# The convolution stage of a two-layer decoder trunk: gating, pivot and mean in PSUM, the first norm among the first products, warm-up products, 26 in place of 18 taps on TensorE

## The chip, the core and the metric

The kernel runs on one core of a Trainium2 chip. The metric is device time in microseconds (us) of one execution. TensorE (PE) multiplies, PEld is its weight load, VectorE (DVE), ScalarE (ACT) and GpSimd (POOL) do the elementwise work, SyncE (SP) issues most DMAs. [...]

## What is computed

A trunk of two layers on 512 tokens of 1024 channels, in float32. Only the first part of layer 0 is touched, the Conformer convolution module behind an RMS norm:

```python
def conformer_conv(h, w_pw1, b_pw1, w_dw, b_dw, ln_g, ln_b, w_pw2, b_pw2):
    u = h @ w_pw1 + b_pw1                     # h = rms_norm(x): 1024 -> 2048
    a, gate = jnp.split(u, 2, axis=-1)
    u = a * jax.nn.sigmoid(gate)
    u = lax.conv_general_dilated(u, w_dw[:, None, :], ..., padding=((30, 0),),
                                 feature_group_count=D_MODEL) + b_dw   # depthwise, causal, 31 taps
    u = jax.nn.silu(layer_norm(u, ln_g, ln_b))
    return u @ w_pw2 + b_pw2                  # added to x
```

Behind it come memory cross-attention, a SwiGLU FFN, and the second layer (differential attention, memory attention, FFN, final norm). Keys and values of the 256 memory tokens do not depend on the convolution, and the kernel computes those of both layers inside the convolution stage.

## The kernel before

Channels lie on the 128 partitions in eight blocks (`KT = 8`), the 512 tokens along the free axis. Each float32 product is three TensorE products: every operand is split into a rounded part (a cast on ACT) and a remainder (a subtraction, `lo`, on DVE or POOL), and `mm3` issues high by high, high by low, low by high (512 columns each). `weights` (L208) loads 128 columns of a matrix, 512 KB, through SP and splits it: cast `wh` at L213 on ACT, remainder `wl` at L215 on the engine given as `lo`.

The order of instructions on each engine is made when the program is built: a scheduler simulates the engines and takes the first ready instruction in program order. `tc.issue_after(x)` keeps the instructions of its block behind `x` on x's engine. At run time each engine works through its own list strictly in order, and semaphores hold an instruction until its inputs are there.

The convolution stage, in `conformer`:

- **Head.** Eight blocks `xT[t]` are loaded, scaled by the norm's gain and split (`Norm.take`: `xg`, cast on ACT L226, remainder on DVE L227). `gated(0)` makes the gate product `pg` of block 0 (8 input blocks, 24 products), squares `x` (ACT L309, sum on DVE L310), sums over channels on TensorE (`sums`, L117 to `ps_st`), then makes the other product `pa`. `spread` forms 1/rms: `rsqrt` takes a POOL power (L269) and one Newton step of three DVE operations (L275 to L277), four transposes (L121) broadcast it, and ACT copies it to `R`. All gating waits for `R`.
- **Gating** of block j (L368 to L371): DVE multiplies `pg` by `R` into `tg`; ACT takes the sigmoid `sg`; DVE multiplies `pa` by `R` into `u[j]` in SBUF (L370) and then forms `(u + bias) * sg` in place (L371), with two SBUF inputs.
- **Convolution** of block j, `conv(j)`: DVE adds tap after tap into a PSUM bank `ps_conv` (L405, one SBUF and one PSUM input); taps 1 to 6 (`POOL_TAPS`) go by ACT (L387) and POOL (L388) into `g`; for blocks 6 and 7 the taps listed in `PE_TAPS` go by TensorE, each tap as a diagonal matrix built on ACT (L398, two operations) and three products. L407 adds `ps_conv` and `g` into `u[j]`.
- **Layer norm.** `pivm` (all 1/1024) times `u[j]` on TensorE gives the mean of blocks 0 to 3 in `pm[0]` (called `ps_piv` in the trace). ACT copies twice that to SBUF as `piv`; `deviations` subtracts it (L414, blocks 0 to 5 on POOL, 6 and 7 on DVE), squares on ACT and adds into `ss` (L420). At the end `mq` (L447) is the mean of what is left, in SBUF; `ss` is corrected (L449), summed on TensorE, `rsqrt` with three Newton steps runs on DVE (L271 to L277), transposes to `ps_bc` broadcast it; `mq` is subtracted from every block (L458: blocks 0 to 2 POOL, 3 to 7 DVE), then L463 scales, ACT takes silu and L220/L221 split for the second pointwise product `ps_out`.
- **Fill.** `memory_kv` is a generator of 32 steps (`ps_mk`, `ps_mv` products); `FILL[j]` steps are taken after block j, and what is left comes after the last mean product `centre`. Its weights use POOL for `wl`.

PSUM has eight banks in this stage: ring 0 to 3 for the pointwise and memory products, 4 and 5 for `ps_conv`, 6 for `piv`, 7 for `st`.

## Time and profile before

| what | us |
|---|---|
| median of 3 runs (lowest to highest) | 1526.03 (1525.06 to 1527.97) |
| the profiled execution's own time | 1527.41 |
| its span, first to last instruction | 1525.6 |
| mean granted TensorE clock | 0.99 of full speed |
| start of the uninterrupted `ps_out` products, which end the stage | 241.84 |

The span is 1.8 us under the profiled execution's own time, and that execution is 1.4 us above the median. Times in the rows are microseconds from the first instruction unless marked ns. Busy matmuls overlap in the records, so the pace of TensorE is read from the chain of waits (a stretch divided by its count), not from the mean of one. [...]

### The profile page before, as it was taken

The numbers are of one execution on the slowest core, as the hardware profiler recorded it, in microseconds if no ns is written. First come the engines' busy times: TensorE is split into PE (matmuls) and PEld (weight loads), VectorE is DVE, ScalarE is ACT, GpSimd is POOL, SyncE is SP. The second block draws the span as 40 slices with busy tenths as digits, with TensorE's granted clock in tenths as the row PEclk, the third lists the DMA queues.
The fourth block names the chain that finished last, engine by engine and source line by source line (L and its number), as shares of the span: only waits on it lengthen the run. The fifth ranks groups of instructions, "written<-read, shape, count | busy, mean of one in ns | idle before, by whom it ended". The sixth has DMA issues, their size and how long they took to land.

```text
span 1525.6 us, 18451 instructions
## 1 busy us (share of the span) xinstructions
PE 1480.9 (97%) x7204; PEld 1213.1 (80%) x7204; DVE 905.2 (59%) x1369; ACT 607.5 (40%) x990; POOL 385.6 (25%) x218
## 2 busy tenths in 40 slices
PE   6999879999999999999999999999999999999998
PEld 4888758887888888888887878788878888888886
DVE  5999986555664345425569888765564533543444
ACT  6655746354343122222334555453443232222222
POOL 5999784310221022012000000011002201210212
PEclk9999999999999999999999999999999999999999
DMA  7454225211433332332323111232124223232321
GB/s 216 125 146 131 93 97 152 69 56 49 121 97 97 88 102 87 98 96 87 93 86 95 56 56 56 86 88 77 56 83 125 89 92 97 87 106 84 97 96 56
DMA packets 231815, 143.59 MB, mean 94 GB/s; under 512 B 5552, under 2 KB 217648, under 8 KB 231728
## 3 DMA queue, kind: packets, MB, share of 16 engines
q1 hardware_dynamic: 230432, 141.58, 31.3%
q8 instruction: 56, 0.92, 0.2%
q10 hardware_dynamic: 1296, 0.84, 0.2%
q14 instruction: 31, 0.25, 0.1%
HBM read 138.20 MB, written 4.19 MB: 93 GB/s over the span
## 4 chain that ended last, share of the span: by engine, by line
PE 88%; DVE 8%; issue 1%; ACT 1%; DMA 1%; POOL 0%; POOLq 0%; DVEq 0%; SPq 0%; ACTq 0%
PE ps_gu L117 32%; PE ps_out L117 9%; PE ps_down L117 8%; PE ps_fin L117 8%; PE ps_lin L117 5%; PE ps_pw L117 3%; PE ps_v L117 3%; PE ps_q L117 3%; PE ps_k L117 2%; PE ps_mv L117 2%; PE ps_mk L117 2%; DVE ps_conv L405 2%; PE ps_s L117 2%; PE ps_mo L117 2%; PE ps_ms L117 1%
## 5 line engine op out<-in xcount | busy, mean ns | idle before, releaser
L213 ACT CAST wh<-st 128x1024 fp32r<-128x1024 f32 (+1 forms) x254 | 263.4, 1041 | 598.3 <-issue 187.2
L117 PE MATMUL ps_gu<-xg,wh 128*128 128x512 f32 x1408 | 438.9, 392 | 0.0
L215 POOL TENSOR_TENSOR wl<-st,wh 128x1024 fp32r<-128x1024 f32 x100 | 258.4, 2590 | 670.5 <-ACT wh L213 637.2
L117 PEld LDWEIGHTS ps_gu<-xg,wh 128*128 128x128 f32 x1408 | 264.3, 188 | 63.0
L117 PE MATMUL ps_gu<-xg,wl 128*128 128x512 f32 x704 | 278.4, 395 | 0.0
L215 DVE TENSOR_TENSOR wl<-st,wh 128x1024 fp32r<-128x1024 f32 (+1 forms) x154 | 186.5, 1214 | 84.1 <-ACT wh L213 81.9
L117 PEld LDWEIGHTS ps_gu<-xg,wl 128*128 128x128 f32 x704 | 132.2, 188 | 28.5
L405 DVE SCALAR_TENSOR_TENSOR ps_conv<-u,wcol,ps_conv 128x499 f32<-128x499 f32 (+21 forms) x176 | 120.1, 730 | 5.3 <-PE ps_conv L117 2.0
L584 DVE TENSOR_TENSOR tu<-ps_gu,R 128x512 f32<-128x512 f32 x44 | 30.4, 691 | 140.0 <-PE ps_gu L117 139.9
L117 PE MATMUL ps_fin<-wh,a 128*128 128x512 f32 (+1 forms) x364 | 111.0, 386 | 0.0
L117 PE MATMUL ps_down<-a,wh 128*128 128x512 f32 x352 | 109.5, 394 | 0.0
L117 PE MATMUL ps_pw<-xg,wh 128*128 128x512 f32 x256 | 84.1, 407 | 12.0 <-ACT wh L213 8.9
L221 DVE TENSOR_TENSOR a<-ta,a 128x512 fp32r<-128x512 f32 x44 | 73.7, 1676 | 22.2 <-ACT a L220 22.2
L117 PE MATMUL ps_lin<-xg,wh 128*128 128x512 f32 x256 | 81.5, 395 | 0.0
L117 PE MATMUL ps_out<-mo,wh 128*128 128x512 f32 x256 | 80.6, 396 | 0.9 <-ACT wh L213 0.9
L117 PEld LDWEIGHTS ps_fin<-wh,a 128*128 128x128 f32 x364 | 67.7, 188 | 15.3
L117 PEld LDWEIGHTS ps_down<-a,wh 128*128 128x128 f32 x352 | 66.0, 188 | 15.2
L582 DVE TENSOR_TENSOR tg<-ps_gu,R 128x512 f32<-128x512 f32 x44 | 30.4, 691 | 76.1 <-PE ps_gu L117 70.2
L117 PE MATMUL ps_fin<-wl,a 128*128 128x512 f32 (+1 forms) x182 | 70.4, 387 | 0.0
L117 PE MATMUL ps_down<-a,wl 128*128 128x512 f32 x176 | 68.8, 394 | 0.0
L117 PEld LDWEIGHTS ps_pw<-xg,wh 128*128 128x128 f32 x256 | 49.0, 195 | 24.7 <-ACT wh L213 8.9
L117 PEld LDWEIGHTS ps_out<-mo,wh 128*128 128x128 f32 x256 | 47.3, 188 | 13.6 <-ACT wh L213 3.4
(256 smaller groups left out, 2517.6 us busy)
## 6 DMA issues: line engine op xcount, KB each, us to landing
st<-in_ffn_w_up_dram SPq DMA_DIRECT2D x44, 512.0 KB, 3.8
st<-in_ffn_w_gate_dram SPq DMA_DIRECT2D x44, 512.0 KB, 3.8
st<-in_ffn_w_down_dram SPq DMA_DIRECT2D x38, 512.0 KB, 3.8
st<-in_conv_w_pw_dram SPq DMA_DIRECT2D x24, 512.0 KB, 4.6
st<-in_mem_w_k_dram SPq DMA_DIRECT2D x16, 512.0 KB, 4.1
st<-in_mem_w_v_dram SPq DMA_DIRECT2D x16, 512.0 KB, 3.7
st<-in_mem_w_q_dram SPq DMA_DIRECT2D x16, 512.0 KB, 4.0
st<-in_mem_w_o_dram SPq DMA_DIRECT2D x16, 512.0 KB, 4.0
```

Source lines behind the costliest of these rows:

```text
L117: ins = nc.tensor.matmul(*args, **kw)
L213: A.copy(wh, st)
L215: (lo or V).tensor_tensor(wl, st, f(wh), op=ALU.subtract)
L221: (lo or V).tensor_tensor(l, src, f(h), op=ALU.subtract)
L405: V.scalar_tensor_tensor(acc[:, s:], u[j][:, :S - s], wt(s), acc[:, s:], op0=ALU.mult, op1=ALU.add)
L582: V.tensor_tensor(tg, pg, n.R, op=ALU.mult)
L584: V.tensor_tensor(tu, pu, n.R, op=ALU.mult)
```

## The change

Six edits, all in the convolution stage.

1. The second half of the gating stays in PSUM: `pa` is multiplied by `R` in place and L371's counterpart has one PSUM and one SBUF input.
2. `pm[0]` gets a bank of its own (ring 6, 7 for `piv`; `st` moves to bank 5, shared with `ps_conv`) and is no longer copied; all eight deviations are DVE operations that read it from PSUM, with the factor -2 in the instruction.
3. The mean is kept in PSUM: ACT copies `pm[1]` to `mq`, DVE puts the difference into `pm[0]`, and all eight final subtractions are DVE operations that read it there.
4. The first norm: the products of blocks 0 and 1 come before both gatings; `sums` comes after `pg` and six of eight input blocks of `pa`, `spread` after three more of block 1; its `rsqrt` runs on DVE with three Newton steps; the two weight remainders of block 0 go to DVE.
5. 48 products of 128 columns in bfloat16 on constants, into a PSUM bank that nothing reads, before the first products.
6. `PE_TAPS`: 10 taps in place of 6 for block 6, 16 in place of 12 for block 7. Taps 2, 4 and 6 of both blocks thereby leave ACT and POOL, tap 18 of block 6 and tap 30 of block 7 leave DVE.

```diff
--- before.py
+++ after.py
@@ -37,7 +37,8 @@
 FFN_GROUPS = [list(range(0, 8)), list(range(8, 16)), list(range(16, 22))]
 NEG = -1.0e30
 POOL_TAPS = [1, 2, 3, 4, 5, 6]
-PE_TAPS = {6: [0, 8, 10, 12, 14, 16], 7: [0, 8, 10, 12, 14, 16, 18, 20, 22, 24, 26, 28]}
+PE_TAPS = {6: [0, 2, 4, 6, 8, 10, 12, 14, 16, 18], 7: list(range(0, CW, 2))}
+WARM = 48
 FILL = [4, 5, 2, 2, 1, 2, 2, 6]
 getcontext().prec = 60
@@ -71,7 +72,7 @@
 MEMB = {"e": 4, "sq": 1, "mo": 16}
 FFN0B = {"tg": 3, "sg": 3, "tu": 4, "ta": 4, "sq": 2, "ctab": 2, "stab": "ctab", "lq": 2, "lpr": "lq", **TABLES}
 FFNB = {"tg": 3, "sg": 3, "tu": 4, "ta": 4, "sq": 2, "gf": 2, "xo": 8}
-CONV = {"mkf": 8, "piv": 2, "mq": "piv", "tg": 2, "sg": 2, "g": 2, "q": 2, "z": "tg", "s_": "sg", "dq": 2,
+CONV = {"mkf": 8, "mq": 1, "tg": 2, "sg": 2, "g": 2, "q": 2, "z": "tg", "s_": "sg", "dq": 2,
         "lss": 1, "msrc": 2, "mks": "msrc", "sq": "dq", "u": 8}
 SLOTS = {
     "c": CONV, "c2": CONV, "m0": {"mkf": 8, **MEMB}, "m1": {"fetch": 4, **MEMB}, "f0": FFN0B, "f1": FFNB,
@@ -87,7 +88,7 @@
 MEMP = {"lin": "01", "ms": "23", "out": "04152637", "": "4567"}
 FFNP = {"": "01234567"}
-CONVP = {"": "0123", "conv": "45", "piv": "6", "st": "7", "bc": "4", "out": "012356"}
+CONVP = {"": "0123", "conv": "45", "piv": "67", "st": "5", "bc": "4", "out": "012356"}
 BANKS = {
     "c": CONVP, "c2": CONVP,
     "m0": MEMP, "m1": MEMP, "f0": FFNP, "f1": FFNP,
@@ -320,12 +321,12 @@
             self.ps = bank("st", [P, NB, 2])
             return token_sums(self.ps, self.ss)
-        def spread(self):
+        def spread(self, eng=G):
             ps = self.ps
             v = small("nv", [P, NB])
             V.tensor_scalar(v, ps[:, :, 0], 1.0 / D, RMS_EPS, op0=ALU.mult, op1=ALU.add)
             self.r = tl("rs", [P, NB])
-            V.tensor_copy(self.r, rsqrt(v, NB))
+            V.tensor_copy(self.r, rsqrt(v, NB, eng))
             pb = bank("st")
             ins = broadcast_rows(self.r, pb)
             self.R = tl("R")
@@ -350,25 +351,50 @@
         for t in range(KT):
             nc.sync.dma_start(xT[t], xt[t * P:(t + 1) * P, :])
             if t == 0:
-                w0 = weights(conv_w_pw1[0][:, D:D + P], lo=G)
+                w0 = weights(conv_w_pw1[0][:, D:D + P])
             n0.take(t, xT[t])
+        warm = bank("piv")
+        for _ in range(WARM):
+            T.matmul(warm[:, :P], identb, mask, start=True, stop=True)
         def gated(j):
             pg, pa = bank("pw1"), bank("pw1")
-            linear(conv_w_pw1[0], KT + j, n0.xs, pg, lo=G, w=w0 if j == 0 else None)
+            W, lo = conv_w_pw1[0], V if j == 0 else G
+            wg = w0 if j == 0 else weights(W[:, (KT + j) * P:(KT + j + 1) * P], lo=lo)
+            wa = weights(W[:, j * P:(j + 1) * P], lo=lo)
+            def product(ps, w, ks):
+                for k in ks:
+                    mm3(ps, at(w, ALLP, k), n0.xs[k], k == 0, k == KT - 1)
             if j == 0:
+                product(pg, wg, range(KT))
+                product(pa, wa, range(6))
                 for t in range(KT):
                     n0.square(xT[t])
-                with tc.issue_after(n0.sums()):
-                    linear(conv_w_pw1[0], j, n0.xs, pa, lo=G)
-                cur["spread"] = n0.spread()
+                cur["sums"] = n0.sums()
+                with tc.issue_after(cur["sums"]):
+                    product(pa, wa, range(6, KT))
+            elif j == 1:
+                with tc.issue_after(cur["sums"]):
+                    product(pg, wg, range(3))
+                cur["spread"] = n0.spread(V)
+                with tc.issue_after(cur["spread"]):
+                    product(pg, wg, range(3, KT))
+                    product(pa, wa, range(KT))
             else:
-                linear(conv_w_pw1[0], j, n0.xs, pa, lo=G)
+                product(pg, wg, range(KT))
+                product(pa, wa, range(KT))
+            return lambda: gate(j, pg, pa)
+        def gate(j, pg, pa):
             tg, sg, uj = tl("tg"), tl("sg"), tl("u")
             V.tensor_tensor(tg, pg, n0.R, op=ALU.mult)
             cur["gate"] = A.activation(sg, tg, AF.Sigmoid, bias=pc("bpw1", KT + j)).ins
-            V.tensor_tensor(uj, pa, n0.R, op=ALU.mult)
-            V.scalar_tensor_tensor(uj, uj, pc("bpw1", j), sg, op0=ALU.add, op1=ALU.mult)
+            V.tensor_tensor(pa, pa, n0.R, op=ALU.mult)
+            V.scalar_tensor_tensor(uj, pa, pc("bpw1", j), sg, op0=ALU.add, op1=ALU.mult)
             return uj
@@ -382,11 +408,13 @@
             g = tl("g")
             G.tensor_copy(g[:, 0:1], pc("bdw", j))
             A.activation(g[:, 1:], u[j][:, :S - 1], AF.Identity, scale=wt(1), bias=pc("bdw", j))
+            taps = PE_TAPS.get(j, [0])
             for s in POOL_TAPS[1:]:
+                if s in taps:
+                    continue
                 q = tl("q")
                 A.activation(q[:, s:], u[j][:, :S - s], AF.Copy, scale=wt(s))
                 G.tensor_tensor(g[:, s:], g[:, s:], q[:, s:], op=ALU.add)
-            taps = PE_TAPS.get(j, [0])
             if j in PE_TAPS:
                 up = split(u[j], "up")
                 for t0 in range(0, len(taps), 4):
@@ -408,10 +436,10 @@
-        pm, piv, ss = [bank("piv"), None], tl("piv"), tl("lss")
+        pm, ss = [bank("piv"), None], tl("lss")
         def deviations(j, eng):
-            eng.tensor_tensor(u[j], u[j], piv, op=ALU.subtract)
+            V.scalar_tensor_tensor(u[j], pm[0], -2.0, u[j], op0=ALU.mult, op1=ALU.add)
             if j == 0:
                 A.activation(ss, u[j], AF.Square)
             else:
@@ -421,13 +449,15 @@
         half = KT // 2
         kv = memory_kv()
-        u = [gated(0)]
+        first = [gated(0), gated(1)]
+        u = [first[0]()]
         for j in range(KT):
             if j == 0:
+                u.append(first[1]())
                 with tc.issue_after(cur["spread"]):
-                    u += [gated(1), gated(2)]
+                    u.append(gated(2)())
             elif j + 2 < KT:
-                u.append(gated(j + 2))
+                u.append(gated(j + 2)())
             if j == 2:
                 w = wcol[:, KT - len(PE_TAPS):, :]
                 G.tensor_copy(wsplit[0], w)
@@ -435,7 +465,6 @@
             conv(j)
             centre = T.matmul(pm[j // half], pivm, u[j], start=j % half == 0, stop=j % half == half - 1)
             if j == half - 1:
-                A.activation(piv, pm[0], AF.Copy, scale=2.0)
                 pm[1] = bank("piv")
                 for jj in range(half):
                     deviations(jj, G)
@@ -444,8 +473,9 @@
             for _ in range(FILL[j]):
                 next(kv)
         mq, q2 = tl("mq"), tl("dq")
-        V.scalar_tensor_tensor(mq, piv, -0.5, pm[1], op0=ALU.mult, op1=ALU.add)
-        A.activation(q2, mq, AF.Square)
+        A.copy(mq, pm[1])
+        V.tensor_tensor(pm[0], mq, pm[0], op=ALU.subtract)
+        A.activation(q2, pm[0], AF.Square)
         squares = V.scalar_tensor_tensor(ss, q2, -float(D // P), ss, op0=ALU.mult, op1=ALU.add)
         pst = bank("st", [P, NB, 2])
         token_sums(pst, ss)
@@ -455,7 +485,7 @@
         broadcast_rows(rsqrt(var, NB, V), pR)
         with tc.issue_after(squares.ins):
             for j in range(KT):
-                (G if j < 3 else V).tensor_tensor(u[j], u[j], mq, op=ALU.subtract)
+                V.tensor_tensor(u[j], u[j], pm[0], op=ALU.subtract)
         phase("c2")
         sl = []
         for j in range(KT):
```

## Rows read from the trace of the kernel before

**Rows 1.** Busy time by stretch: us, busy us (instructions) per engine, granted clock.

```profile
0.00:34.00 34.00, 18.78 (x62) 13.15 (x63) 20.26 (x26) 19.12 (x33) 18.63 (x22) 0.90 0.83 237
34.00:155.00 121.00, 121.00 (x688) 104.67 (x686) 115.30 (x154) 70.12 (x94) 116.88 (x70) 1.00 0.44 129
155.00:212.00 57.00, 52.13 (x230) 42.14 (x230) 50.33 (x63) 37.00 (x73) 49.93 (x31) 0.94 0.27 88
212.00:242.00 30.00, 20.33 (x83) 16.16 (x82) 25.59 (x28) 14.06 (x19) 19.10 (x8) 0.83 0.51 146
242.00:1525.60 1283.60, 1268.69 (x6148) 1036.95 (x6146) 693.69 (x1101) 467.21 (x774) 181.07 (x90) 1.00 0.29 86
```

**Rows 2.** TensorE's waits, 0 to 245 us: who waited for whom, total, times, longest.

```profile
PE ps_pw L117 <- ACT wh L213: 8.9, 1, 8.9
PE ps_bc L121 <- DVE ry L277: 8.6, 1, 8.6
PE ps_piv L117 <- DVE u L407: 4.9, 1, 4.9
PE ps_pw L117 <- DVE xg L227: 3.0, 3, 2.4
PE ps_st L117 <- DVE ss L310: 2.0, 1, 2.0
PE ps_pw L117 <- POOL wl L215: 1.2, 1, 1.2
```

**Rows 3.** Granted clock, same columns as Rows 1, short stretches around two waits.

```profile
26.00:28.30 2.30, 2.30 (x6) 1.74 (x6) 0.66 (x2) 0.00 (x0) 2.30 (x3) 0.50 0.63 171
162.00:164.00 2.00, 2.00 (x11) 2.00 (x11) 1.96 (x5) 2.00 (x5) 1.28 (x1) 0.50 0.00 0
230.00:232.00 2.00, 2.00 (x6) 1.55 (x5) 1.70 (x3) 1.42 (x3) 0.00 (x0) 0.50 0.00 0
```

**Rows 4.** Chain that ended last, pieces in order of time: start, duration, what.

```profile
23.88 1.87 PE ps_st L117 x8
33.37 0.44 PE ps_st L121 x4
33.80 22.10 PE ps_pw L117 x96
175.92 2.80 PE ps_mv L117 x12
178.72 5.43 PE ps_conv L117 x24
228.55 10.55 PE ps_mv L117 x36
```

**Rows 5.** DVE groups, 0 to 245 us: busy us, mean ns of one.

```profile
L371 DVE SCALAR_TENSOR_TENSOR u<-u,prm,sg 128x512 f32<-128x512 f32 x8 | 21.8, 2730 | 1.3 <-ACT sg L369 1.3
L458 DVE TENSOR_TENSOR u<-u,mq 128x512 f32<-128x512 f32 x5 | 12.9, 2631 | 0.0
L447 DVE SCALAR_TENSOR_TENSOR mq<-piv,ps_piv 128x512 f32<-128x512 f32 x1 | 0.7, 675 | 0.0
L405 DVE SCALAR_TENSOR_TENSOR ps_conv<-u,wcol,ps_conv 128x499 f32<-128x499 f32 (+21 forms) x176 | 120.1, 730 | 5.3 <-PE ps_conv L117 2.0 <-ACT ps_conv L402 1.6
```

**Rows 6.** Page, costliest groups: remainder of a weight block on DVE.

```profile
L215 DVE TENSOR_TENSOR wl<-st,wh 128x1024 fp32r<-128x1024 f32 (+1 forms) x154 | 186.5, 1214 | 84.1 <-ACT wh L213 81.9
```

**Rows 7.** Timeline, DVE and POOL: start, duration, engine, instruction, idle before it.

```profile
142.61 10.35 DVE L371 SCALAR_TENSOR_TENSOR u<-u,prm,sg 128x512 f32<-128x512 f32 x1
142.66 1.29 POOL L388 TENSOR_TENSOR g<-g,q 128x508 f32<-128x508 f32 x1
145.16 4.76 POOL L215 TENSOR_TENSOR wl<-st,wh 128x1024 fp32r<-128x1024 f32 x2
28.76 1.24 DVE L275 TENSOR_TENSOR rb<-nv,ry 128x4 f32<-128x4 f32 x1 [2.11 <-POOL ry L269]
30.23 0.16 DVE L277 SCALAR_TENSOR_TENSOR ry<-rb,ry 128x4 f32<-128x4 f32 x1
```

## The prediction

> **What bounds the kernel now.** The first view is busy time by stretch [rows 1]. Behind 242 us TensorE is busy for 1268.69 of 1283.60 us at a granted clock of 1.00: the change touches nothing there, and that part can only shift as a whole. So the question is when the convolution stage ends, and before that TensorE loses time in three places: the first 34 us (18.78 busy), 155 to 212 (52.13 of 57) and 212 to 242 (20.33 of 30, clock 0.83). The second view, TensorE's waits up to 245 us [rows 2], names them. The waits shown add up to 28.6 us: 8.9 for the first weights, 6.2 more in the head (xg 3.0, ss 2.0, wl 1.2), 4.9 for u of block 4 and 8.6 for the reciprocal root of the layer norm. [...] In the chain, 36 memory products behind the last wait took 10.55 us, 0.293 each, where 12 of the same kind took 2.80 earlier, 0.233 each: 2.2 us lost [rows 4].
>
> Why DVE was late is read from its groups [rows 5]. L371, with two SBUF inputs, takes 2730 ns on average; L447 and L405, of the same size but with one input in PSUM, take 675 and 730, with POOL just as busy. The timeline shows the mechanism: one L371 lasted 10.35 us while POOL ran subtractions and additions without a gap, and a DVE operation on four elements took 1.24 us beside POOL and the like 0.16 a moment later [rows 7]. DVE operations with two SBUF inputs wait for POOL. From 34 to 155 us DVE is busy 115.30 and POOL 116.88 of 121 us [rows 1], TensorE all of it, since the memory products fill its gaps: three engines at their limit at once.
>
> [...]
>
> **The change part by part.** The sum is in time TensorE loses, since the stage ends when TensorE is through.
>
> Gating in PSUM: eight L371 go from 2.73 us to about 0.7 (L447 and L405): 16 us less on DVE [rows 5]. Two taps fewer take off 2 x 0.73. Six more deviations and three more final subtractions add 9 x 0.7 = 6.3, but the five final ones that were on DVE fall from 2.63 to 0.7, 9.6 less, and those lay on the path. POOL loses six tap additions, six deviations, three subtractions and two weight remainders: 15 x 1.29 + 2 x 2.38 = 24 us [rows 7] (a weight remainder is half of the 4.76). So from the first gating to the last convolution sum DVE's list, about 160 us of work now, shrinks by some 13 us net, and POOL's by as much, while TensorE's list grows: TensorE alone sets the pace, DVE and POOL have slack.
>
> [...]
>
> *Head.* Now 48 `ps_pw` products are done at 33.80 us, when the broadcast ends; 57 would be done at 33.80 + 9 x 0.230 = 35.9 [rows 4]. After the change 57 products lie ahead of the broadcast. The first still waits 8.9 us for its weights. Then the list is bound by the squares: ACT and DVE have to make eight splits and eight squares, now with two weight remainders more on DVE (1.2 us each [rows 6]), but without POOL beside the first of them. I take the sums to end where they end now, 25.75 [rows 4]; TensorE has 42 products (9.7 us) to do until then, which fit. Behind them 15 products take 3.5 us and cover the reciprocal root, some 0.7 + 12 x 0.2 = 3.1 us if nothing blocks it. So the broadcast starts at 29.2 in place of 33.37, and 57 products are done at 29.2 + 0.4: **6.3 us gained**, with ends of 2 (its nine two-input operations wait for POOL as L275 did, 1.1 us each for four of them) and 9.5 (sums at 22.5, since DVE is not held up early).
>
> *Warm-up.* [...] What they give is the clock of the first products, which are bound by their inputs for the most part: taken as nothing, ends -1.5 and +0.5.
>
> *Middle wait.* 4.9 us, and then about 5 us at 0.50 that lose half, 2.5. It goes if DVE is not late, and with gating 5 us earlier and 14 us of L371 contention gone by then, it has that several times over: **7.4 gained**. What is late next is TensorE itself.
>
> *Added taps.* 8 x 3 products at 5.43/24 = 0.226 [rows 4]: **5.4 lost**, in full, since TensorE is then the bound. 16 more diagonals on ACT against six fewer tap products there: ACT is busy 37 of 57 us there [rows 1], nothing. The next chunk of diagonals waits for two buffers; TensorE waits then if ACT is late, bounded by about 1 us.
>
> *Layer norm.* Now 1.0 to 1.2 for a weight, 8.6 for the root, 2.2 to 2.6 of clock: 12. The five contended subtractions (12.9 us) sat in front of the root; eight uncontended ones take 8 x 0.62 = 5. But the root's nine two-input operations and L449 now meet POOL, which has weight remainders for the memory products to make; a wait of one such instruction is up to 2.4 us. It limits itself: when TensorE stops, POOL gets no free buffers and stops too, as in the wait before. I take 5 left over (ends 0 and 11): **7.3 gained**, ends 1 and 12. The memory products that remain behind the last mean cover the chain of the norm otherwise.
>
> The moved bank of `st` (5, shared with `ps_conv`) and the two banks of `piv` add waits only where a convolution sum of block 1 or 7 is still being read; both lie many microseconds off: nothing, at worst 1. Holding `pa` in PSUM until L371 is done keeps a bank some 1 to 2 us longer, and the ring comes round to it after four groups of products of 5.5 us (24 x 0.230): nothing.
>
> Sum: 6.3 + 7.4 - 5.4 + 7.3 = **15.6 us** off the profiled 1527.41, 1511.8; that execution is 1.4 above the median, so the forecast for the median is **1510.4**.
>
> **The rivals.**
> - *The contention moves to the small operations, some.* Both roots wait for POOL at most steps: head gains 2, norm gains 1, the middle 7.4, taps 5.4 lost: 5 us, 1521. For it: L275 [rows 7]. Against it: in the head POOL is idle for a good part. [...]
> - *Slower: the first norm stalls everything.* `issue_after` puts all later products behind the broadcast, so if POOL runs back to back, each of the nine operations waits a whole remainder of 2.4 us: 21 us in place of 3, the broadcast at 47 against 33.4 now. Head 13 us lost, taps 5.4 lost, 14.7 gained: +4, 1530. It decides from about 1.5 us for each operation on (9 x 1.3 more than the cover). Against it: POOL is busy for 18.63 of the first 34 us [rows 1] and loses work there.
> - *DVE or POOL still sets the pace*, so that the middle wait stays in part: 10 us gained, 1516.
> - *All waits go*: head 9.5, warm clock 1.5, middle 7.4, norm 11, taps 5.4: 24 us, 1502.
> - *It does not do what it says*: the planner puts the first sums no earlier and the warm-up does not raise the clock. Then head 2: 1514, within the range.
>
> **How the numbers follow.** Forecast (with the last rival) 0.62, moved contention 0.15, slower 0.07, DVE or POOL 0.08, all gone 0.08. The range leaves the slower case and the ends of the others out: 1501 to 1521. What this kernel's measurement can tell from no change is about 0.2%, 3 us. Only the slower case and the worse end of moved contention fall outside faster: faster 0.89, same 0.05, slower 0.06.
>
> **What would show it.** L371's counterpart and the final subtractions at 0.7 us; the first broadcast near 29 us; no TensorE wait between 30 and 180 us over 1 us and a clock of 1.00 there; a wait for the second root of about 5 us; the `ps_out` run that starts at 241.84 now starting near 226, and everything behind it unchanged. I am wrong if L275 to L277 take more than 1 us each, or if TensorE waits for DVE or POOL in the middle, or if the stretch behind the stage changes its length.

## The result and the profile after

The changed kernel takes 1503.03 us (median of 4 runs, 1502.42 to 1503.75) against 1527.00 us on the same chips: a ratio of 0.9844, 95% interval 0.9827 to 0.9861. That is 7.4 us below the forecast of 1510.4, 2 us above the lower end of its range. Its profiled execution took 1502.42 us with a span of 1500.6. Lines have moved: products stand at L118, transposes at L122, the cast of a weight block at L214 and its remainder at L216, the splits at L222 and L228, the root at L272 to L278, the second half of the gating at L397, a deviation at L442, the final subtraction at L488.

The spans differ by 25.0 us (1525.6 and 1500.6). The trace splits that by the first products of each part of the program; "first behind" is the first `ps_lin` product, with which the convolution stage is over.

| us | before | after | difference |
|---|---|---|---|
| convolution stage, up to the first product behind it | 285.5 | 271.8 | 13.7 |
| memory attention of layer 0 | 118.4 | 118.6 | -0.2 |
| FFN of layer 0 | 368.5 | 364.9 | 3.6 |
| `ps_q` products of layer 1 | 45.8 | 45.5 | 0.3 |
| attention of layer 1 | 208.4 | 205.7 | 2.7 |
| memory attention of layer 1 | 119.9 | 118.9 | 1.0 |
| FFN of layer 1 and final norm | 379.1 | 375.3 | 3.8 |

So 13.7 us come out of the stage and 11.3 out of code that the change does not touch.

Busy time by stretch, after (columns as in [rows 1], which it answers):

```profile
0.00:34.00 34.00, 25.29 (x120) 18.95 (x121) 21.39 (x36) 20.70 (x35) 16.76 (x21) 0.90 0.90 253
34.00:155.00 121.00, 121.00 (x705) 106.16 (x704) 112.06 (x168) 74.06 (x109) 109.03 (x66) 1.00 0.43 129
155.00:212.00 57.00, 57.00 (x254) 45.68 (x253) 46.62 (x71) 34.66 (x68) 38.41 (x21) 1.00 0.30 96
212.00:242.00 30.00, 28.03 (x121) 21.90 (x120) 16.33 (x20) 19.81 (x27) 12.92 (x6) 1.00 0.67 195
```

Between 155 and 212 us TensorE loses nothing now (57.00 of 57, 52.13 before), DVE has 10 us free there and POOL 19. From 34 to 155 DVE and POOL went down by 3 and 8 us and TensorE is the bound, as before. TensorE's waits up to 245 us, after (answering [rows 2]):

```profile
PE ps_pw L118 <- DVE xg L228: 4.2, 4, 3.3
PE ps_piv L118 <- DVE identb L197: 1.8, 1, 1.8
PE ps_out L118 <- DVE sl L222: 1.8, 2, 1.1
PE ps_pw L118 <- ACT wh L214: 1.3, 1, 1.3
PE ps_out L118 <- POOL wl L216: 0.8, 1, 0.8
PE ps_st L118 <- DVE ss L311: 0.7, 1, 0.7
```

The waits for `u` of the middle (4.9) and for the layer norm's root (8.6) are gone. What is left lies in the head, above all one of 3.3 us for `xg`, and among the first `ps_out` products, which now wait for their own inputs and weights. The groups on DVE (answering [rows 5]; busy us, mean ns of one):

```profile
L397 DVE SCALAR_TENSOR_TENSOR u<-ps_pw,prm,sg 128x512 f32<-128x512 f32 x8 | 6.0, 745 | 1.3 <-ACT sg L395 1.3
L442 DVE SCALAR_TENSOR_TENSOR u<-ps_piv,u 128x512 f32<-128x512 f32 x8 | 5.2, 686 | 6.1 <-PE ps_piv L118 6.1
L488 DVE TENSOR_TENSOR u<-u,ps_piv 128x512 f32<-128x512 f32 x8 | 4.9, 678 | 0.0
```

With one input in PSUM the gating takes 745 ns on average where it took 2730, the final subtraction 678 where it took 2631. And the granted clock where it stood at 0.50 at 162 and 230 us in [rows 3]:

```profile
162.00:164.00 2.00, 2.00 (x10) 1.66 (x9) 1.97 (x4) 0.69 (x2) 2.00 (x3) 1.00 0.67 237
226.00:232.00 6.00, 4.87 (x20) 3.49 (x19) 4.03 (x5) 5.14 (x8) 3.10 (x2) 1.00 0.95 283
```

The head is the one part that did not come out as worked out. Timeline of the squares' sums on DVE, of POOL beside them, and of TensorE, after (start, duration, idle time ahead in brackets):

```profile
16.62 5.51 POOL L216 TENSOR_TENSOR wl<-st,wh 128x1024 fp32r<-128x1024 f32 x2 [10.20 <-ACT wh L214]
16.99 2.90 DVE L228 SCALAR_TENSOR_TENSOR xg<-xT,prm,xg 128x512 fp32r<-128x512 f32 x1
19.81 2.86 DVE L311 TENSOR_TENSOR ss<-ss,sq 128x512 f32<-128x512 f32 x1
24.40 0.54 PE L118 MATMUL ps_pw<-xg,wh 128*128 128x512 f32 x1 [3.28 <-DVE xg L228]
26.08 1.87 PE L118 MATMUL ps_st<-ones,ss 128*128 128x2 f32 x8 [0.72 <-DVE ss L311]
33.05 0.60 PE L122 MATMUL ps_st<-ident,rs 128*128 128x128 f32 x4
```

Outside the stage, the chain of waits gives the pace of the longest uninterrupted runs of TensorE in the first FFN (start, duration, count), before:

```profile
495.12 44.47 PE ps_down L117 x192
539.59 88.81 PE ps_gu L117 x384
```

and after:

```profile
480.42 44.22 PE ps_down L118 x192
524.64 87.66 PE ps_gu L118 x384
```

The same 384 products, without a wait in either kernel and at a clock of 1.00, take 0.2313 us each before and 0.2283 after. This is where 7.4 us of the FFNs come from (3.6 and 3.8 in the table). Nothing in the prediction accounts for it.

### The profile page after: what moved, and what is told of

It reads as the page before. It is cut to its first block, busy times and chain, and to the rows that moved or that the text cites. A ratio compares the mean times of both kernels' runs of the same rounds, so it can differ in the third digit from the quotient of the medians.

```text
span 1500.6 us, 18604 instructions
## 1 busy us (share of the span) xinstructions
PE 1476.0 (98%) x7276; PEld 1216.6 (81%) x7276; DVE 885.3 (59%) x1386; ACT 609.1 (41%) x1000; POOL 356.3 (24%) x200
## 4 chain that ended last, share of the span: by engine, by line
PE 93%; DVE 3%; ACT 1%; issue 1%; DMA 1%; POOL 0%; POOLq 0%; DVEq 0%; ACTq 0%
PE ps_gu L118 32%; PE ps_out L118 10%; PE ps_down L118 8%; PE ps_fin L118 8%; PE ps_lin L118 6%; PE ps_pw L118 5%; PE ps_mk L118 3%; PE ps_q L118 3%; PE ps_v L118 3%; PE ps_mv L118 2%; PE ps_k L118 2%; PE ps_s L118 2%; PE ps_part L118 2%; PE ps_mo L118 2%; PE ps_ms L118 2%; PE ps_conv L118 1%
## 5 line engine op out<-in xcount | busy, mean ns | idle before, releaser
L214 ACT CAST wh<-st 128x1024 fp32r<-128x1024 f32 (+1 forms) x254 | 263.8, 1042 | 608.5 <-issue 173.2
L118 PE MATMUL ps_gu<-xg,wh 128*128 128x512 f32 x1408 | 435.3, 390 | 0.0
L216 POOL TENSOR_TENSOR wl<-st,wh 128x1024 fp32r<-128x1024 f32 x98 | 251.0, 2565 | 685.4 <-ACT wh L214 641.1
L118 PEld LDWEIGHTS ps_gu<-xg,wh 128*128 128x128 f32 x1408 | 264.2, 188 | 57.5
L118 PE MATMUL ps_gu<-xg,wl 128*128 128x512 f32 x704 | 275.9, 392 | 0.0
L216 DVE TENSOR_TENSOR wl<-st,wh 128x1024 fp32r<-128x1024 f32 (+1 forms) x156 | 188.7, 1212 | 86.3 <-ACT wh L214 85.7
L118 PEld LDWEIGHTS ps_gu<-xg,wl 128*128 128x128 f32 x704 | 132.2, 188 | 27.8
L433 DVE SCALAR_TENSOR_TENSOR ps_conv<-u,wcol,ps_conv 128x487 f32<-128x487 f32 (+15 forms) x174 | 117.7, 729 | 7.0 <-ACT ps_conv L430 3.0
L118 PE MATMUL ps_fin<-wh,a 128*128 128x512 f32 (+1 forms) x364 | 110.8, 386 | 0.0
L118 PE MATMUL ps_down<-a,wh 128*128 128x512 f32 x352 | 109.1, 392 | 0.0
L118 PE MATMUL ps_pw<-xg,wh 128*128 128x512 f32 x256 | 82.4, 401 | 5.5 <-DVE xg L228 4.2
L222 DVE TENSOR_TENSOR a<-ta,a 128x512 fp32r<-128x512 f32 x44 | 72.4, 1646 | 22.2 <-ACT a L221 22.2
L118 PE MATMUL ps_out<-mo,wh 128*128 128x512 f32 x256 | 81.5, 398 | 0.8 <-ACT wh L214 0.8
L118 PE MATMUL ps_lin<-xg,wh 128*128 128x512 f32 x256 | 81.7, 395 | 0.0
L118 PEld LDWEIGHTS ps_fin<-wh,a 128*128 128x128 f32 x364 | 67.7, 188 | 14.7
L118 PEld LDWEIGHTS ps_down<-a,wh 128*128 128x128 f32 x352 | 66.0, 188 | 14.8
L118 PE MATMUL ps_fin<-wl,a 128*128 128x512 f32 (+1 forms) x182 | 70.1, 386 | 0.0
L118 PE MATMUL ps_down<-a,wl 128*128 128x512 f32 x176 | 68.7, 393 | 0.0
L118 PEld LDWEIGHTS ps_pw<-xg,wh 128*128 128x128 f32 x256 | 48.2, 191 | 17.8 <-DVE xg L228 6.5
L118 PEld LDWEIGHTS ps_out<-mo,wh 128*128 128x128 f32 x256 | 47.2, 188 | 13.5 <-ACT wh L214 3.4
```

The costliest lines, as they stand in the source:

```text
L118: ins = nc.tensor.matmul(*args, **kw)
L214: A.copy(wh, st)
L216: (lo or V).tensor_tensor(wl, st, f(wh), op=ALU.subtract)
L222: (lo or V).tensor_tensor(l, src, f(h), op=ALU.subtract)
L433: V.scalar_tensor_tensor(acc[:, s:], u[j][:, :S - s], wt(s), acc[:, s:], op0=ALU.mult, op1=ALU.add)
```

## The experiments

Two questions: why the same products run at another pace, and what each edit is worth by itself. All "before" medians beside these runs lay between 1525.96 and 1526.81 us.

### Where the pace of the FFN comes from

Every big tile of the kernel is 2048 bytes, or a multiple, in each partition. The small ring tiles (24 of 32 bytes each, and two `rs`, 832 bytes together) are placed wherever the program first asks for them, and every big tile placed behind them is shifted by 832 bytes against those placed ahead. The change asks in another order, because the head is in another order. From the compiled programs, joined to the trace, for the three buffers of each kind of weight tile:

| `ps_gu` products whose weights lie at | offset (address modulo 2048) | mean us of one, before | offset, after | mean us of one, after |
|---|---|---|---|---|
| `wh`, buffer 1 | 288 | 0.2305 | 288 | 0.2269 |
| `wh`, buffer 2 | 288 | 0.2288 | 288 | 0.2284 |
| `wh`, buffer 3 | 1120 | 0.2312 | 288 | 0.2272 |
| `wl`, buffer 1 | 288 | 0.2314 | 288 | 0.2272 |
| `wl`, buffer 2 | 1120 | 0.2333 | 288 | 0.2269 |
| `wl`, buffer 3 | 1120 | 0.2358 | 1120 | 0.2358 |

The moving tiles `xg` lie at 288 in both. After, five of six buffers lie like `xg`; before, three, and two of those (`wh` 1 and `wl` 1) run clearly slower there than after, between their displaced neighbours. Theory: the pace of a product depends on where its moving tile and the weights lie relative to each other. Rival: it is the clock, or other traffic, that differs between the executions.

**b_pad and a_pad.** The kernels before and after, with two more `rs` buffers, so that the shift is 896 bytes, a multiple of 128:

```diff
-GLOBAL = {"R": 2, "rs": 2, "ss": 1, "xg": 16}
+GLOBAL = {"R": 2, "rs": 4, "ss": 1, "xg": 16}
```

> The kernel before, with two more 16-byte buffers of `rs` (64 bytes more), so that every tile of the rings behind it starts at 32 modulo 128 instead of 96; instructions and their order are unchanged. Background: behind the convolution stage the changed kernel also lost 11.3 of its 25 us, with one product taking 0.228 instead of 0.231 us on average. Placement theory: products run at 0.2267 us where weight and moving tile start at the same offset modulo 128 and at 0.230 to 0.236 otherwise, so the stretch of 384 ps_gu products falls from 88.8 to about 87.1 us and the whole from 1526 to about 1508 us, with the same three waits in the convolution stage. Theory of another chip or another clock: 1526 us and 88.8, as before.

> The changed kernel with the same 64 bytes more, all else the same. Placement theory: the one ring slot of weights that still starts at 96 modulo 128 joins the others, 384 ps_gu products fall from 87.7 to about 87.1 us, the whole from 1503 to about 1496 us. Theory that the faster products come from the changed instructions (other positions of the program, other timing): 1503, nothing changes.

Measured: before with the padding 1523.08 us (10 runs, 1521.46 to 1530.01; ratio 0.9991, 0.9974 to 1.0007), after with it 1504.28 (0.9854, 0.9839 to 0.9869). Neither is faster than without by more than the runs spread. The 384 `ps_gu` products take 89.09 and 87.60 us. The theory with a period of 128 bytes falls; a longer period is left open by this.

**b_align and a_align.** The same edit with 40 buffers: the small tiles now fill 2048 bytes (24 x 32 + 40 x 32), and every big tile lies at the same offset of 288.

```diff
-GLOBAL = {"R": 2, "rs": 2, "ss": 1, "xg": 16}
+GLOBAL = {"R": 2, "rs": 40, "ss": 1, "xg": 16}
```

> The kernel before with `rs` in 40 buffers of 32 bytes, so that every tile of the rings, small ones aside, starts at the same offset modulo 2048; instructions and order unchanged. In b_pad and a_pad the offset modulo 128 was made equal and the slow pairs stayed slow, so equality modulo 128 is not the rule; the fast pairs of weight tiles lay a multiple of 4096 bytes apart and at a multiple of 2048 from xg, the slow ones at 64 or 128 modulo 256. Placement theory, second form (equal offset modulo something from 256 to 2048): all ps_gu products at 0.2267 us, 384 in 87.1 us, the whole about 1509 us. Rival (the pace has nothing to do with the offset, it is the distance to what ACT, DVE or DMA write at the time): no clear change from b_pad, 1523.

> The changed kernel with the same. Second form: 384 ps_gu products in 87.1 us against 87.6, the third pair of weight tiles as fast as the others, ps_down at 0.227, the whole about 1497 us. The difference to b_align is then what the change is worth in the convolution stage alone: 12 to 14 us by the stage ends of the traces (285.69 and 271.96 us for the first product behind it). Rival: 1503, as the change.

Measured: before 1508.82 us (1503.29 to 1510.15; ratio 0.9876, 0.9856 to 0.9896), after 1493.27 (0.9778, 0.9762 to 0.9794). The chain of waits of the kernel before with equal offsets:

```profile
490.37 43.53 PE ps_down L117 x192
533.91 87.04 PE ps_gu L117 x384
```

and of the kernel after with equal offsets:

```profile
479.26 43.53 PE ps_down L118 x192
522.79 87.04 PE ps_gu L118 x384
```

Both run at 0.2267 us for a product. No instruction and no order differs from the unpadded kernels, only addresses. So the placement sets the pace: 17.5 us for the kernel before, 9.8 for the one after. The difference of the two, 7.7 us, is what the change gained by a side effect of its new order; the other 15.5 us (1508.82 to 1493.27) remain when both are placed alike.

**a_xg_off.** The kernel a_pad with every `xg` tile 64 bytes longer, so that the moving tiles step through all offsets in 64-byte steps, while the weights stay where they are modulo 256 bytes:

```diff
     def pair(name, shape=(P, 512)):
+        if name == "xg":
+            return tl(name, (P, 528), F32R)[:, :512], tl(name, (P, 528), F32R)[:, :512]
```

> As a_pad, but each xg tile is 64 bytes longer, so that the high parts of the moving operands start at 32 and the low parts at 96 modulo 128; weights all at 32. Same instructions and order. Placement theory: ps_gu products fall back to about 0.231 us, 384 in 88.5 to 89 us, products without xg (ps_down) stay at about 0.227; the whole near 1506 us. Otherwise: as a_pad.

Measured: 1508.71 us (2 runs, ratio 0.9883, 0.9863 to 0.9903), 4.4 us slower than a_pad. Its chain of waits:

```profile
483.53 44.10 PE ps_down L118 x192
527.63 88.49 PE ps_gu L118 x384
```

`ps_gu`, which streams `xg`, goes from 87.60 to 88.49; `ps_down`, which does not, takes 44.10 in both. It is the place of the moving tile against the weights. Sorted by that distance, the products with the first `wh` buffer (about 128 in each group) take 0.2264 us at a distance of 0, 256, 512 or 768, 0.2281 at 64 more, 0.2305 at 128 more, 0.2329 at 192 more: in this buffer the pattern repeats every 256 bytes. It is no general rule. The 0.2305 at 128 is the mean of two paces, 0.2364 where the next product has the same weights and 0.2246 where it has those in `wl`, and with the other two `wh` buffers 128 is the fastest distance (0.2252 and 0.2277). So the weights that are loaded meanwhile count too; which of them, and how, stays open. For b_pad it says that a shift of 896, which is 128 modulo 256, need be no better than 832, which is 64.

### What each edit is worth

All of these start from the kernel after with equal offsets (a_align, 1493.27 us, first product behind the stage at 272.6 us), so that the placement doesn't move with the edit. Two limits hold for what follows. The intervals of the ratios are 0.0014 to 0.0021 to either side, 2 to 3 us, so medians that lie closer together than that do not tell two kernels apart. And the end of the stage comes from one profile each: the kernels after, a_pad and a_align, with the same instructions, end it at 271.8, 271.9 and 272.6 us, at granted clocks of 0.91, 0.86 and 0.81 over the first 36 us, so a difference of about 1 us can be the execution's.

**a_gate_sbuf.** Edit 1 undone, the gating of block j in SBUF again:

```diff
-            V.tensor_tensor(pa, pa, n0.R, op=ALU.mult)
-            V.scalar_tensor_tensor(uj, pa, pc("bpw1", j), sg, op0=ALU.add, op1=ALU.mult)
+            V.tensor_tensor(uj, pa, n0.R, op=ALU.mult)
+            V.scalar_tensor_tensor(uj, uj, pc("bpw1", j), sg, op0=ALU.add, op1=ALU.mult)
```

> a_align (1493.3 us) with the gating's second half in SBUF again, two SBUF inputs for its last operation; all else stays. Contention theory: the eight operations take about 2.5 us each beside POOL, 14 us more on DVE; DVE has idled little in the middle, so TensorE waits there again: 3 to 8 us slower, 1497 to 1501. Theory that TensorE is the bound with slack on DVE: within 1 us.

Measured: 1494.04 us (ratio 0.9788, 0.9772 to 0.9804), the stage ends at 273.4. The DVE group of this kernel:

```profile
L397 DVE SCALAR_TENSOR_TENSOR u<-u,prm,sg 128x512 f32<-128x512 f32 x8 | 19.3, 2408 | 1.3 <-ACT sg L395 1.3
```

Its busy time in the two middle stretches:

```profile
34.00:155.00 121.00, 121.00 (x699) 106.14 (x698) 116.00 (x161) 70.08 (x94) 110.49 (x66) 1.00 0.42 125
155.00:212.00 57.00, 55.80 (x252) 44.59 (x252) 49.35 (x71) 37.69 (x83) 37.28 (x20) 1.00 0.31 97
```

The contention is back (2408 ns) and DVE is busier by 5 us up to 155, but TensorE loses only 1.2 us, 0.7 of it in a wait for a cast on ACT. The edit most visible in the profile is worth 0.8 us, which is within the noise: the 13 us of DVE time lie in its slack.

**a_mean_sbuf.** Edits 2 and 3 undone (the banks stay as after), pivot and mean in SBUF with the subtractions shared between POOL and DVE (the main lines):

```diff
-            V.scalar_tensor_tensor(u[j], pm[0], -2.0, u[j], op0=ALU.mult, op1=ALU.add)
+            eng.tensor_tensor(u[j], u[j], piv, op=ALU.subtract)
...
+                A.activation(piv, pm[0], AF.Copy, scale=2.0)
...
-                V.tensor_tensor(u[j], u[j], pm[0], op=ALU.subtract)
+                (G if j < 3 else V).tensor_tensor(u[j], u[j], mq, op=ALU.subtract)
```

> a_align with pivot and mean in SBUF again: six deviations and three last subtractions on POOL, the copies on ACT and DVE as in the kernel before. Contention theory: the five last subtractions on DVE take 2.6 us each, the root comes some 9 us late, TensorE waits about 8 us and loses 2 more at half rate: 8 to 11 us slower, 1501 to 1504. Rival (the memory products that are left cover the norm in any case): within 2 us.

Measured: 1510.81 us (ratio 0.9897, 0.9883 to 0.9912), the stage ends at 288.8. TensorE's largest waits up to 245 us:

```profile
PE ps_bc L122 <- DVE ry L278: 7.3, 1, 7.3
PE ps_piv L118 <- DVE u L435: 5.8, 1, 5.8
```

and the group of final subtractions that DVE keeps:

```profile
L488 DVE TENSOR_TENSOR u<-u,mq 128x512 f32<-128x512 f32 x5 | 12.9, 2651 | 0.0
```

Both waits of [rows 2] return, the middle one of 5.8 too, although the gating stays in PSUM here. These two edits carry 17.5 us (16.2 by the end of the stage), well above the 8 to 11 of the expectation. The wait for the root has the five subtractions of 12.9 us ahead of it. What makes DVE late for the middle wait is one operation, the split of `u` for the taps on TensorE (L222), with two SBUF inputs; POOL's last instruction beside it stands in the second row:

```profile
143.85 10.40 DVE L222 TENSOR_TENSOR up<-u,up 128x512 fp32r<-128x512 f32 x1 [0.25 <-ACT up L221]
152.38 1.33 POOL L448 TENSOR_TENSOR lss<-lss,dq 128x512 f32<-128x512 f32 x1
```

The same pair in a_gate_sbuf:

```profile
140.92 8.36 DVE L397 SCALAR_TENSOR_TENSOR u<-u,prm,sg 128x512 f32<-128x512 f32 x1
147.46 1.27 POOL L417 TENSOR_TENSOR g<-g,q 128x506 f32<-128x506 f32 x1
```

and the POOL instruction that belongs to the L371 of 10.35 us in [rows 7], in the kernel before:

```profile
151.13 1.29 POOL L420 TENSOR_TENSOR lss<-lss,dq 128x512 f32<-128x512 f32 x1
```

In all three POOL works without a gap meanwhile, and the DVE operation ends some 0.54 us after POOL's last instruction: at 154.25 (POOL 153.71), 149.28 (148.73) and 152.96 (152.42). So how late DVE comes out of it is set by when POOL's unbroken run ends, whichever operation is caught: 5.0 us later here than in a_gate_sbuf, and the wait for `u` is 5.8 in place of 0.5. The four deviations that go back to POOL, 5.07 us from 129.35 on, lengthen that run. Not every operation waits for the end of the run: the same split takes 4.60 us in after (from 142.46, POOL's run to 149.33) and 0.99 in a_align (from 143.61, run to 150.47). And this is read from traces; no run changed POOL's list alone, or edit 2 without edit 3.

**a_head_old.** Edit 4 undone, the old order of the head with `R` spread before block 1, the root by the POOL power and the remainders of block 0 on POOL (the main lines):

```diff
-        first = [gated(0), gated(1)]
-        u = [first[0]()]
+        u = [gated(0)()]
...
-                u.append(first[1]())
                 with tc.issue_after(cur["spread"]):
-                    u.append(gated(2)())
+                    u += [gated(1)(), gated(2)()]
```

> a_align with the head of the kernel before: sums behind the gate product of block 0, reciprocal root by the POOL power, weight remainders of block 0 on POOL; the warm-up products stay. The traces show the broadcast at 33.4 us before and 33.2 after, and 9 products more done by then: 2 us slower, 1495 to 1496. My forecast had 6 us for this edit: 1499.

Measured: 1493.94 us (ratio 0.9791, 0.9777 to 0.9806), the stage ends at 274.1: 1.5 us by the end of the stage, 0.7 by the medians, which is within the noise.

**a_v1.** The kernel a_pad with the weight remainders of block 1 on DVE, to take POOL from beside the sums of squares:

```diff
-            W, lo = conv_w_pw1[0], V if j == 0 else G
+            W, lo = conv_w_pw1[0], V if j <= 1 else G
```

> As a_pad, but the two weight remainders of block 1 are also made on DVE instead of POOL. Contention theory for the head: in the changed kernel four two-input DVE operations between 17 and 26 us took 2.9, 2.9, 1.7 and 1.8 us beside POOL's remainders, 6.5 us too long; DVE gets 2 x 1.2 us more work and loses most of the excess, so the first sums end about 3 us earlier (25 in place of 28), TensorE's 3.3 us wait and half-rate stretch behind it shrink, and the whole falls by 2 to 4 us against a_pad. If ACT's casts or the squares bound the head instead, it does not move by more than 1 us.

Measured: 1506.67 us (ratio 0.9867, 0.9850 to 0.9883), 2.4 us slower than a_pad. The wait for `xg` is gone and the sums are through at 22.9 us in place of some 28, but now the root stands beside POOL. DVE's timeline:

```profile
23.08 1.10 DVE L272 TENSOR_SCALAR ry<-nv 128x4 int32<-128x4 int32 x1
24.21 2.33 DVE L273 TENSOR_SCALAR ry<-ry 128x4 int32<-128x4 int32 x1
26.57 2.25 DVE L276 TENSOR_TENSOR rb<-nv,ry 128x4 f32<-128x4 f32 x1
28.86 0.16 DVE L277 SCALAR_TENSOR_TENSOR rb<-rb,ry 128x4 f32<-128x4 f32 x1
```

and TensorE's largest wait up to 245 us:

```profile
PE ps_st L122 <- DVE rs L329: 6.3, 1, 6.3
```

Operations on four elements take up to 2.33 us. This is the rival "the contention moves to the small operations", which the kernel after itself escaped: there the same twelve steps take 0.16 to 0.32 each, because POOL happens to be idle from 28.47 to 31.45 us.

**a_quiet.** a_align without any POOL subtraction up to the root: block 1, the memory tokens' split and the first two memory weights all on DVE.

```diff
-            W, lo = conv_w_pw1[0], V if j == 0 else G
+            W, lo = conv_w_pw1[0], V if j <= 1 else G
-hl = split(src, "memx", (P, 2, M), lo=G)
+hl = split(src, "memx", (P, 2, M))
-linear(mem_w_k[L], 2 * m2 + mi, memx, ps[:, mi, :], lo=G)
+linear(mem_w_k[L], 2 * m2 + mi, memx, ps[:, mi, :], lo=V if L == m2 == 0 else G)
```

> As a_align, and in the head POOL has no subtraction: the weight remainders of blocks 0 and 1, the splits of the memory tokens and the first two memory weights go to DVE. In a_v1 (block 1 alone moved) the sums ended 5 us earlier, at 22.9 us, but then operations of the reciprocal root on four elements took 1.1 to 2.3 us beside POOL and the broadcast waited 6.3 us. Contention theory: root in about 2.2 us, broadcast near 27 us instead of 33, no TensorE wait over 1.5 us in the head, and the whole 4 to 7 us under a_align. Rival (DVE's longer list delays the first gatings, or later work waits): within 1.5 us of a_align.

Measured: 1494.19 us (ratio 0.9787, 0.9766 to 0.9808), no gain. The broadcast comes at 30.10 in place of 33.64, later than the 27 expected, since two of POOL's remainders now start together with the root (from 23.22 us on). DVE has taken over POOL's work, and a later stretch shows where the gain went: TensorE waits there for a cast on ACT (1.3 us) and for `u` on DVE (1.1). Busy time of a_quiet:

```profile
155.00:200.00 45.00, 42.62 (x181) 33.40 (x179) 38.08 (x54) 30.78 (x67) 30.22 (x18) 1.00 0.24 76
```

and of a_align in the same stretch:

```profile
155.00:200.00 45.00, 45.00 (x206) 36.55 (x205) 33.66 (x46) 27.52 (x57) 29.33 (x17) 1.00 0.24 75
```

2.4 us of the 3.5 are lost again there, and the stage ends at 271.7 against 272.6. Here a gain in the head counted only as far as the engines that paid for it had room up to the end of the convolution.

**a_taps18.** Edit 6 undone, 18 taps on TensorE:

```diff
-PE_TAPS = {6: [0, 2, 4, 6, 8, 10, 12, 14, 16, 18], 7: list(range(0, CW, 2))}
+PE_TAPS = {6: [0, 8, 10, 12, 14, 16], 7: [0, 8, 10, 12, 14, 16, 18, 20, 22, 24, 26, 28]}
```

> a_align with 18 taps on TensorE in place of 26. If TensorE is the bound throughout, 24 products of 0.22 us go: 5.3 us faster, 1488. If the last blocks' taps on DVE, ACT and POOL would then end late, TensorE waits for the last sums instead: no gain or up to 5 us slower, 1493 to 1498.

Measured: 1489.14 us (ratio 0.9762, 0.9748 to 0.9777), the fastest of all kernels here. The stage ends at 267.4, 5.2 us earlier than in a_align; the first `ps_out` product comes 3.8 earlier (220.34 and 224.10), and the other 1.4 arise among the `ps_out` products, where the weights and inputs arrive. TensorE waits 1.9 us for `u` in the middle, as the only price. Its largest wait outside the head:

```profile
PE ps_piv L118 <- DVE u L435: 1.9, 1, 1.9
```

and its busy time around it, where POOL has gone up to 46 us from the 38 of after:

```profile
155.00:212.00 57.00, 55.15 (x250) 44.46 (x249) 47.91 (x71) 34.58 (x62) 46.14 (x28) 1.00 0.34 108
```

So with pivot and mean in PSUM, DVE and POOL have nearly all the room for the eight taps, and giving them to TensorE, the engine that is the bound, costs more than it saves: some 5.4 us of products against the wait of 1.9, which agrees with the 3.8 and with the 4.1 of the medians, though the intervals of the two ratios overlap.

**a_warm0.** Edit 5 undone, no warm-up products:

```diff
-WARM = 48
+WARM = 0
```

> The kernel after with all ring tiles at equal offsets (1493.3 us) and without the 48 warm-up products; nothing else differs. Forecast: the first products are bound by their inputs, so 0 to 1.5 us slower, 1493 to 1495 us, with the first real product still at 8.4 us but at a granted clock of 0.50 (0.43 us each) for its first few us. Rival, that the warm-up carries more than the forecast says, since the first squares and sums wait for TensorE: 3 us or more slower, 1496 us or above. Rival that it costs something: the first real product starts earlier than 8.4 us without it.

Measured: 1491.95 us (ratio 0.9772, 0.9755 to 0.9788), 1.3 below a_align, within what the intervals leave open; the stage ends at 269.8. The clock in two stretches of the head without the warm-up:

```profile
6.00:12.00 6.00, 3.91 (x8) 2.57 (x9) 4.71 (x7) 5.94 (x13) 0.01 (x1) 1.00 1.08 357
24.00:34.00 10.00, 9.43 (x34) 7.42 (x35) 4.22 (x15) 3.36 (x5) 6.38 (x4) 0.66 0.57 158
```

and with it (a_align):

```profile
6.00:12.00 6.00, 3.88 (x18) 2.70 (x16) 4.64 (x7) 5.94 (x12) 1.02 (x2) 0.77 1.08 359
24.00:34.00 10.00, 9.41 (x30) 7.34 (x30) 4.26 (x15) 2.61 (x3) 6.38 (x4) 0.54 0.57 161
```

Without the warm-up the first product starts at 8.06 us, with it at 8.13, and the broadcast comes at 32.6 and 33.6: the products are bound by their inputs either way. The half clock behind the 3.3 us wait ends some 2 us earlier in this profile without it (at 31 us, with it at 33), and that 1.0 us stays up to 223 us; the other 1.8 arise among the `ps_out` products, where the weights arrive. Neither can be put down to the edit: over the first 36 us the granted clock is 0.91 here, and 0.91, 0.86 and 0.81 in the profiles of after, a_pad and a_align, which all have the warm-up. That the warm-up gains or costs anything is not shown.

## Why the prediction was right, and where it was not

The sign and the range held. The sum of the stage was near (13.7 us by the two profiles, 15.6 forecast), but by other shares, whose errors cancel, and the time beyond it has a cause outside the steps. That the whole still lies in the range of 1501 to 1521 is luck in part: the 11.3 us from behind the stage, which the forecast had at nothing, brought it to 2 us from the lower end.

| step | forecast, us | undone alone: end of the stage | medians |
|---|---|---|---|
| gating in PSUM (edit 1) | with pivot and mean 14.7 | 0.8 | 0.8 |
| pivot and mean (edits 2, 3) | see above | 16.2 | 17.5 |
| head (edit 4) | 6.3 | 1.5 | 0.7 |
| warm-up (edit 5) | 0 | -2.8 | -1.3 |
| taps (edit 6) | -5.4 | -5.2 | -4.1 |
| sum | 15.6 | 10.5 | 13.6 |
| all together, placed alike | 15.6 | 11.1 (283.7 to 272.6) | 15.5 |

- **Middle wait.** It went, by the mechanism that was named: in the kernel before, the L371 of 10.35 us caught beside POOL stands ahead of it. The step that failed is the cure: "It goes if DVE is not late, and with gating 5 us earlier and 14 us of L371 contention gone by then, it has that several times over". With the gating back in SBUF, L371's counterpart takes 8.36 us and the wait for `u` is only 0.5; with pivot and mean back it is 5.8 though the gating is quick, because another operation with two SBUF inputs is caught in its place for 10.40. So what the rows speak for is the work taken off POOL, more than the one operation taken out of its way. The rest of DVE's 13 us in L371 lay ahead of 155 us, where TensorE had memory products to fill with. The 2.5 us in the 7.4 that were put down to the clock stand in the trace of before: behind the wait it is 0.50 from 159.9 to 165.0 us, where after has 1.00 from 155 to 242.
- **Layer norm.** Sized too low: 5 us of the root wait were to be left over, and none is. The memory products cover the whole chain from the last mean to the first broadcast (`ps_bc` at 215.2 us without a wait). With the clock at 1.00 the 12 us of [rows 2, 3] are gained in full, the forecast's upper end. What is late next is new: the weights and inputs of `ps_out`. Its first product starts 15.4 us earlier (238.9 to 223.5), although ten memory products that stood behind it before (2.3 us at 0.233) now stand ahead. From there to the end of the stage it takes 48.3 us in place of 44.2 without those ten: some 4 are lost again, 2.6 of them in waits of 1.8 and 0.8 us, a term that the forecast did not have.
- **Head.** The step "I take the sums to end where they end now, 25.75" failed. They end at 27.95, 2.2 us later, because L228 and L311 beside POOL's two remainders take 2.90 and 2.86 us, and the next two beside its split 1.74 and 1.76, where they take 0.74 and 0.68 alone. The wait of 3.28 us that it makes is followed by the half clock (0.50 from 24.7 to 31.5 us), so the 15 products behind the sums take from 27.81 to 33.05, 5.2 in place of 3.5: another 1.7. Together they are the 3.9 us by which the broadcast is later than the 29.2 of the forecast. The root itself was as worked out (27.99 to 30.68, 2.7 us against 3.1). The prediction had weighed this contention only for the nine small operations, not for the larger ones ahead of them.
- **Warm-up.** Nothing, as forecast; these runs show no effect that stands out of the noise. That the warm-up raises the clock of the first products was the author's assumption, and no run shows it: from 6 to 12 us the granted clock is 1.00 in a_warm0, 1.00 in after and 0.77 in a_align.
- **Taps.** Forecast 5.4 lost "in full". Measured are 5.2 by the stage, 4.1 by the medians and 3.8 by the first `ps_out` product. The 24 products cost that much, but without them 1.9 us of the middle wait come back, so "in full" was somewhat too much.
- **"Everything behind it unchanged"** failed: 11.3 us. The prediction had itself named a change there as a sign of being wrong. 7.4 are the pace of the FFNs by the placement, shown by b_align and a_align. The rest lies for the most part in layer 1's attention and memory attention. There short waits of 0.7 us are in some executions followed by a stretch of half clock and in others not; in the profile of before one of them is, at 981 us:

```profile
981.00:984.00 3.00, 3.00 (x9) 2.26 (x8) 2.46 (x6) 1.17 (x5) 0.08 (x1) 0.50 0.17 43
```

  and in the profile of after none. The same stretch of attention takes 205.5 to 208.9 us in the kernels here without any order by edit (a_align 207.1, a_warm0 205.5, a_mean_sbuf 205.6, b_align 208.9), so these 3.7 us are more likely of the execution than of the change; which it is was not shown. Between the profiles of b_align and a_align 4.6 us lie in these two parts as well (1.8 and 2.8), so 11 us is a better figure for the change in the stage than the 15.5 of the medians.
- **The rivals.** "All waits go" gave 1502, the measured time, but not by its terms: the head gained 1.5 to 2.2 and not 9.5, and the placement made up for it. "The contention moves to the small operations" was seen in a_v1 and a_quiet, which differ from the kernel after only in the engine of a few remainders and splits. "The first norm stalls everything" did not decide, since POOL was idle from 28.47 to 31.45 us.

In a_quiet the contention reached operations with one input too: L272 and L273 take 2.41 and 2.28 us beside two POOL remainders that take 4.73 together, and L276 behind them 0.16. The prediction had counted operations with two SBUF inputs only.

## What to carry to other kernels

Before a slow group is blamed for a wait, ask which one of its operations stands ahead of the wait, and what that one waited for: here the operation changed from kernel to kernel, and how long it took hung on when the other engine's unbroken run ended. Taking eight operations out of the contention was worth 0.8 us, taking work off the engine that they contend with, and off the path to the root, 16. When the bound has moved to one engine, work that was once moved to it should be moved back and timed again (the taps: about 4 us). And where the same instructions run at another pace in a part that was not touched, compare the addresses of their tiles before looking for anything else.

## What the runs showed of the hardware

A `ps_gu` product of 512 columns took 0.2267 us on average where all moving tiles and weights start at equal offsets (b_align, a_align), and up to 0.236 in the kernels before and after; in a_xg_off the four distances of 64 bytes gave 0.2264, 0.2281, 0.2305 and 0.2329 us for one weight buffer and another order for the others. Placed so by 1216 bytes of padding, the kernel before gains 17.5 us without a change of any instruction, more than the six edits give in their stage (11.1 placed alike, 13.7 as they were), and with the edits and 18 taps the kernel runs in 1489.14 us. That version without the warm-up was not run.

A DVE operation of 128x512 with two SBUF inputs, 0.68 to 0.74 us alone, took 8.36, 10.35 and 10.40 us where POOL worked without a gap, and ended some 0.54 us after POOL's last instruction. Single-input operations on four elements took up to 2.41 us beside POOL in place of 0.17 to 0.32.
